# One place sooner: context sum and root between the query's products, a tile's column sums ahead of the bias columns, and the first weights rounded on VectorE

## The chip, the cores and the metric

The kernel runs on one core of a Trainium2 chip. A core has five engines that run side by side, each with its own instruction queue, in order: TensorE (PE in the rows; its weight loads are PEld), VectorE (DVE), ScalarE (ACT), GpSimd (POOL) and SyncE (SP), which here issues most of the transfers. Engines wait for each other at semaphores. The metric is the device time of one execution in microseconds, lower is better.

## The reference

One layer of a diffusion backbone over 512 latent tokens and 256 context tokens with 1024 channels. Only the start matters here:

```python
mod = silu(c) @ w_mod + b_mod                      # six pieces; here shift and scale 1
mod_c = silu(c_ctx) @ w_mod + b_mod
h_lat = rmsnorm(x, norm1_g) * (1 + sc1) + sh1      # 512 x 1024
h_ctx = rmsnorm(ctx, norm1_g) * (1 + csc1) + csh1  # 256 x 1024
p_lat, p_ctx = h_lat @ w_in, h_ctx @ w_in
```

The columns of `w_in` feed a state-space mixer, a windowed attention whose latent queries also read the context's keys and values, and two gates. A merge, a gated convolution FFN and a last norm follow.

## The kernel before

**Products in two parts.** Every fp32 operand of a large product is split into a rounded part `hi` and a remainder `lo`, and a product is three TensorE passes: hi x hi, hi x lo, lo x hi. Weights are split by `split(r, n, hi, lo)` (L148): a ScalarE copy rounds into `hi` (L149), a VectorE subtraction gives `lo` (L150). Activations are channel-major, in eight tiles of 128 channels: `hlh`, `hll` for the latent tokens, `hch`, `hcl` for the context.

**The opening stage.** Eight tiles j = 0 to 7 of the input are worked on while their modulation weights `wm` (two transfers of 512 KB for each j) and the first gate's weights `w0` (five column blocks of 128) stream in on SP's queue. For each tile the steps of the order below are:

- `A`: sixteen small products of `silu(c)` with the modulation weights (L370), copied by ScalarE to a row `tm` (L372); here also `split_w(j)` splits the gate weights of the tile into `w0h` and `w0l`.
- `B`: four small products that turn the row into columns (L380), and two ScalarE steps that make the tile's scale `a` (L381) and shift `s` (L382) from them. These are the column sums of the tile.
- `H`: the tile's operand. For j below 4 it is `x` times the scale alone (`scaled`: ScalarE `ah` L409, VectorE `al` L410), as the norm's root is not there yet; from j = 4 on it is the whole norm (`norm`: VectorE L400 on `xsb`, ScalarE `hlh` L401, VectorE `hll` L402).
- `Pj:ab`: the products of tile j with the gate's column blocks a to b-1 (L418), accumulated in five PSUM banks.
- `Z`: for j below 4, the shift's own product with the gate weights (L427), a bias.
- `N`: the full norm of tiles 0 to 3, later.
- `sum_l`, `put_l`: TensorE sums the squares (L237), VectorE and GpSimd make the root (L247, L248), TensorE spreads it over the partitions (L254) and ScalarE copies it out as `r_l` (L273). `scale_a`, `scale_b` multiply the five banks by it (L455). `sum_c` and `put_c` do the same for the context: squares `sq_c`, `sq_d` (ScalarE L393, VectorE L395 into `te`), then the sum, the root and `r_c`.
- `rows`, `cols`: the gate's bias, taken out of PSUM as rows by ScalarE (L459, L460) and turned into columns by small products (L464, L465), which ScalarE copies to `gb` (L467).
- `hold`, `keep`: products that nobody reads.

**What sets the order.** TensorE's order in this stage is the written one. The other engines' instructions are placed by the framework's planner, from its own estimate of what is ready when, with the program's order as rank. After the last tile comes the query's first gemm, still in written order: eight steps k of three products (L193, L194, L196). `gemm` takes one entry from the list `BETWEEN` after steps 1, 4 and 7:

```python
if BETWEEN and k % 3 == 1:
    BETWEEN.pop(0)()
```

Behind it, ScalarE's tanh (L533) empties the five gate banks, `norm` makes the context's `hch`, `hcl` from `r_c`, and `k_step` multiplies the key weights with latent and context operands; the planner orders TensorE again there. The query's rotation reads its bank through four ScalarE swaps (L612) and a VectorE product (L616), and the second query tile and the values follow. The attention and the later stages have orders of their own, written out or made by a planner inside the kernel with fixed costs.

Of the kernel before, what the change touches and what calls it, by code (L numbers as in the profile page):

```python
# [13 lines left out]
ALU = mybir.AluOpType  # L14
# [25 lines left out]
def raw(ap):  # L40
    return ap.bitcast(F32)
# [3 lines left out]
def tile_hybrid_layer(  # L45
# [33 lines left out]
    V, S, G, T = nc.vector, nc.scalar, nc.gpsimd, nc.tensor  # L79
# [28 lines left out]
    def accb():  # L108
        return bank("acc")
# [37 lines left out]

    def split(r, n, hi, lo):  # L148
        S.copy(hi[:, :n], r[:, :n])  # L149
        V.tensor_tensor(lo[:, :n], r[:, :n], raw(hi[:, :n]), ALU.subtract)  # L150

    ELSEWHERE = {}

    def load(key):
        r, n = load_raw(key)
        if key[0] == "m":
            return r
        if key in ELSEWHERE:
            hi, lo = ELSEWHERE[key]()
            split(r, n, hi, lo)  # L160
            return hi, lo
        hi = wpool.tile([P, 1024], F32R, tag="whi", name="whi", bufs=2)
        lo = wpool.tile([P, 1024], F32R, tag="wlo", name="wlo", bufs=2)
        split(r, n, hi, lo)
        return hi, lo
# [19 lines left out]
    BETWEEN = []  # L185

    def gemm(targets, w, nk=KT, m=P, k0=0, first=True, last=True, ks=None):
        hi, lo = w
        for k in range(nk) if ks is None else ks:
            wh, wl = hi[:, k * m : (k + 1) * m], lo[:, k * m : (k + 1) * m]  # L190
            a, b = first and k == 0, last and k == nk - 1
            for ps, xh, xl in targets:
                T.matmul(ps, wh, xh[:, k0 + k, :], start=a, stop=False)  # L193
                T.matmul(ps, wh, xl[:, k0 + k, :], start=False, stop=False)  # L194
            for ps, xh, xl in targets:
                T.matmul(ps, wl, xh[:, k0 + k, :], start=False, stop=b)  # L196
            if BETWEEN and k % 3 == 1:
                BETWEEN.pop(0)()
# [13 lines left out]
    half = cpool.tile([P, NV - V_CW], F32, name="half")  # L212
# [87 lines left out]
    with tc.tile_pool(name="spool", bufs=1) as sp:  # L300
# [15 lines left out]
        def load_w0(j):  # L316
            r = sp.tile([P, 640], F32, tag="w0", name="w0", bufs=4)
            nc.sync.dma_start(r, w0[j])
            return r
# [11 lines left out]
        w0_raw = {0: load_w0(0)}  # L331
# [31 lines left out]
        def mod_rows(j):  # L363

            for u in range(2):
                i = 2 * j + u
                w = mod_raw.pop(i) if i in mod_raw else load_mod(i)
                for k in range(4):
                    z = slice(32 * k, 32 * k + 32)
                    T.matmul(pmod[z, 0:256], csil32[:, 4 * u + k, :], w[:, k, :], start=u == 0, stop=u == 1)  # L370
            row = tmp("tm")[:, :256]
            tc.keep_in_program_order(S.copy(row, pmod[:, 0:256]))  # L372
            if j + 1 < KT and j + 1 not in w0_raw:
                w0_raw[j + 1] = load_w0(j + 1)
            W[j] = split_w(j)
            return row
# [7 lines left out]
        def split_w(j):  # L384
            hi = sp.tile([P, 640], F32R, tag="w0h", name="w0h", bufs=2)
            lo = sp.tile([P, 640], F32R, tag="w0l", name="w0l", bufs=2)
            split(w0_raw[j], 640, hi, lo)
            return hi, lo

        def squares(x_, q, n, ks):  # L390
            for k in ks:
                sq = tmp(("ta", "tb")[k % 2])[:, :n] if k else q
                tc.keep_in_program_order(S.activation(sq, x_[:, k, :], AF.Square))  # L393
                if k:
                    V.tensor_tensor(q, q, sq, ALU.add)  # L395
# [17 lines left out]
        def products(j, w, h, gs=range(NG)):  # L413

            st, en = j == 0, j in (NU - 1, KT - 1)
            for a, b in ((0, 0), (0, 1), (1, 0)):
                for i in gs:
                    T.matmul(  # L418
                        pg[i], w[a][:, i * P : (i + 1) * P], h[b], start=st and a + b == 0, stop=en and a == 1,
                        skip_group_check=True,  # L420
                    )
# [10 lines left out]
        r, W, H = {}, {}, {}  # L432
# [16 lines left out]
        def hold(n):  # L449
            for _ in range(n):  # L450
                T.matmul(unread[:, :256], still[:, :P], still, start=True, stop=True)
# [21 lines left out]
        def load_next():  # L473
# [9 lines left out]
        rows = {}  # L483
# [7 lines left out]
        calls = {  # L491
            "sq_0": lambda: squares(xs_, ssq, L, range(1)),
            "sq_1": lambda: squares(xs_, ssq, L, range(1, 2)),
            "sq_2": lambda: squares(xs_, ssq, L, range(2, 4)),
            "sq_3": lambda: squares(xs_, ssq, L, range(4, 8)),
            "hold": lambda: hold(18),
            "keep": lambda: hold(6),
            "sq_c": lambda: squares(xc_, cq, LC, range(4)),
            "sq_d": lambda: squares(xc_, cq, LC, range(4, 8)),
# [13 lines left out]

        order = """
            hold A0 keep B0 H0 sq_0 keep Z0 P0:02 A1 P0:23 B1 H1 sq_1 P0:35 A2 P1:02 B2 H2 sq_2 P1:25 Z1 P2:02 sq_3 A3 P2:23 B3 H3
            P2:35 sum_l Z2 P3:02 A4 put_l P3:23 B4 H4 P3:35 scale_a Z3 scale_b rows A5 half P4:02 cols P4:23 B5 H5 P4:35 A6
            P5:02 B6 H6 P5:24 A7 ctx N0 P5:45 B7 H7 next P6:02 N1 P6:25 N2 P7:02 sq_c N3 P7:25 sq_d
        """
        with tc.manual_schedule(engines={mybir.EngineType.PE}):
            for what in order.split():  # L520
                if what in calls:
                    calls[what]()
                elif what[0] == "P":
                    j = int(what[1])
                    products(j, W[j], H[j], range(int(what[3]), int(what[4])))
                else:
                    does[what[0]](int(what[1]))
            first["q"] = accb()
            BETWEEN.extend([lambda: None, calls["sum_c"], calls["put_c"]])
            gemm([LAT(first["q"])], first["w"][0])  # L530
        for i in range(NG):
            t = tmp("tb")
# [1625 lines left out]
```

## Time and profile before

| | before |
|---|---|
| median of 3 runs | 1234.06 us (1233.9 to 1234.56) |
| the profiled execution | 1233.26 us |
| its span, first to last instruction | 1231.3 us |
| granted TensorE clock, mean | 0.998 |
| TensorE busy | 1217.0 us (99% of the span) |
| VectorE, ScalarE, GpSimd busy | 913.9, 687.9, 168.0 us |

The profile is one execution. A row of the timeline has the start in us from the span's start, the duration, engine, line, operation, output and inputs with their shapes, the count where neighbours are merged, and in brackets the idle time of the engine before it with what ended it. A row of the list of waits has the engine, tile and line that waited, the one it waited for, then us in total, times and the longest. A row of the table of windows has the window's bounds, its length, the busy time (and count) of TensorE, its weight loads, VectorE, ScalarE and GpSimd, then the granted clock, the DMA engines' busy share and GB/s. A row of the chain has start, duration and the work that the end of the span is traced back to. Ends of products are modelled and overlap, so the steps between starts say more than durations.

### The profile page before, as it was taken

To read this page: it belongs to the slowest core of one execution; us is meant where nothing else is said; L and a number is where in the kernel's file an instruction comes from. 1 tells how busy PE (TensorE), PEld (TensorE's weight loads), DVE (VectorE), ACT (ScalarE), POOL (GpSimd) and SP (SyncE) were. 2 spreads that over 40 slices of the span, in tenths; PEclk is the share of its full clock that TensorE was granted. 3 is DMA by queue.
4 is the path that set the end of the run, shared out by engine and by line. 5 is a ranking of instruction groups with operands and counts; after the bars stand their busy time and mean duration, and the time that the engine had idled before them with its cause. 6 is when DMAs were issued, how large, how long until landed. Compare 5 with 4: busy or idle time off the path is not lost.

```text
span 1231.3 us, 17460 instructions
## 1 busy us (share of the span) xinstructions
PE 1217.0 (99%) x6328; PEld 996.2 (81%) x6328; DVE 913.9 (74%) x1483; ACT 687.9 (56%) x1303; POOL 168.0 (14%) x174
## 2 busy tenths in 40 slices
PE   9999999999999999999999999999999999999997
PEld 6788888888878877777777778888988888888886
DVE  4767887888664698697886786677688788886566
ACT  4657788888444646566586563223544444445543
POOL 0000111121100043233351530000200000000000
PEclk9999999999999999999999999999999999999999
DMA  9653668877946235445346466677144444457785
GB/s 357 254 146 89 211 191 193 222 191 204 229 148 213 87 122 144 127 127 183 128 134 203 135 200 226 226 249 233 47 164 150 145 151 150 153 170 250 240 318 183
DMA packets 108630, 224.65 MB, mean 182 GB/s; under 512 B 9600, under 2 KB 48832, under 8 KB 108544
## 3 DMA queue, kind: packets, MB, share of 16 engines
q1 hardware_dynamic: 101056, 197.32, 48.6%
q0 software_dynamic: 6912, 25.17, 8.8%
q8 instruction: 50, 0.82, 0.3%
q10 hardware_dynamic: 576, 1.05, 0.2%
q14 instruction: 36, 0.29, 0.1%
HBM read 193.29 MB, written 49.87 MB: 197 GB/s over the span
## 4 chain that ended last, share of the span: by engine, by line
PE 93%; DVE 3%; ACT 2%; DMA 1%; issue 0%; SPq 0%; POOLq 0%; ACTq 0%; DVEq 0%
PE acc L193 19%; PE acc L194 19%; PE acc L196 19%; PE acc L1915 3%; PE acc L1913 3%; PE acc L1914 3%; PE score L807 3%; PE po L856 3%; PE pt L843 2%; PE mis L418 2%; PE mis L1476 2%; PE mis L1381 2%; PE acc L926 1%; PE acc L927 1%; PE acc L928 1%; PE mis L1399 1%
## 5 line engine op out<-in xcount | busy, mean ns | idle before, releaser
L193 PE MATMUL acc<-hlh,whi 128*128 128x512 f32 x488 | 199.3, 408 | 0.0
L150 DVE TENSOR_TENSOR wlo<-wraw,whi 128x1024 fp32r<-128x1024 f32 (+2 forms) x119 | 143.5, 1207 | 72.3 <-ACT whi L149 62.7
L149 ACT CAST whi<-wraw 128x1024 fp32r<-128x1024 f32 (+2 forms) x119 | 122.8, 1033 | 128.2 <-PE acc L194 80.1
L196 PE MATMUL acc<-hlh,wlo 128*128 128x512 f32 x488 | 191.4, 392 | 0.0
L194 PE MATMUL acc<-hll,whi 128*128 128x512 f32 x488 | 190.7, 391 | 0.0
L193 PE MATMUL acc<-mh,whi 128*128 128x512 f32 x360 | 141.0, 392 | 0.0
L196 PE MATMUL acc<-mh,wlo 128*128 128x512 f32 x360 | 140.1, 389 | 0.0
L194 PE MATMUL acc<-ml,whi 128*128 128x512 f32 x360 | 140.0, 389 | 0.0
L196 PEld LDWEIGHTS acc<-hlh,wlo 128*128 128x128 f32 x488 | 91.6, 188 | 20.3
L194 PEld LDWEIGHTS acc<-hll,whi 128*128 128x128 f32 x488 | 91.9, 188 | 17.5 <-issue 1.7
L193 PEld LDWEIGHTS acc<-hlh,whi 128*128 128x128 f32 x488 | 91.8, 188 | 17.5 <-issue 2.2
L193 PEld LDWEIGHTS acc<-mh,whi 128*128 128x128 f32 x360 | 67.6, 188 | 14.4 <-issue 0.5
L194 PEld LDWEIGHTS acc<-ml,whi 128*128 128x128 f32 x360 | 67.6, 188 | 14.3 <-issue 0.5
L196 PEld LDWEIGHTS acc<-mh,wlo 128*128 128x128 f32 x360 | 67.6, 188 | 14.2
L816 DVE CUSTOM_DVE_ANT_0 p<-score,winm,nsink 128x512 f32<-128x512 f32 (+1 forms) x64 | 51.8, 810 | 15.1 <-PE score L807 13.6
L1264 DVE SCALAR_TENSOR_TENSOR ta<-acc,half,ta 128x511 f32<-128x511 f32 (+1 forms) x66 | 43.8, 663 | 25.7 <-ACT ta L1263 25.6
L1263 ACT ACTIVATE ta<-acc,half 128x512 f32<-128x512 f32 (+1 forms) x66 | 46.7, 708 | 27.0 <-PE acc L196 25.7
L1271 ACT ACTIVATE tb<-ta 128x512 f32<-128x512 f32 (+1 forms) x44 | 23.5, 534 | 65.2 <-DVE ta L1265 59.2
L823 ACT ACTIVATE p<-p,mneg 128x512 f32<-128x512 f32 (+1 forms) x64 | 49.7, 777 | 15.3 <-DVE mneg L816 14.7
L1383 POOL TENSOR_TENSOR st<-st,eT 128x512 f32<-128x512 f32 x24 | 33.5, 1396 | 170.2 <-ACT st L1401 161.9
L193 PE MATMUL acc<-hch,whi 128*128 128x256 f32 x176 | 54.5, 310 | 1.2 <-ACT hch L401 1.2
L851 DVE TENSOR_TENSOR ptl<-pt,pth 128x512 fp32r<-128x512 f32 x72 | 47.5, 686 | 8.6 <-ACT pth L847 7.8
(501 smaller groups left out, 2969.4 us busy)
## 6 DMA issues: line engine op xcount, KB each, us to landing
wraw<-wup SPq DMA_DIRECT2D x44, 512.0 KB, 3.6
wt_d<-wdn POOLq DMA_DIRECT2D x36, 512.0 KB, 7.5
fb<-cs_d SPq DMA_DIRECT2D x32, 512.0 KB, 6.4
wraw<-wm SPq DMA_DIRECT2D x32, 512.0 KB, 4.2
wraw<-wx SPq DMA_DIRECT2D x24, 512.0 KB, 3.6
wraw<-wt_d SPq DMA_DIRECT2D x20, 512.0 KB, 4.2
sp_d<-te SPq DMA_DIRECT2D x33, 256.0 KB, 2.3
wm<-wm SPq DMA_DIRECT2D x16, 512.0 KB, 7.7
```

The costliest lines, as they stand in the source:

```text
L149: S.copy(hi[:, :n], r[:, :n])
L150: V.tensor_tensor(lo[:, :n], r[:, :n], raw(hi[:, :n]), ALU.subtract)
L193: T.matmul(ps, wh, xh[:, k0 + k, :], start=a, stop=False)
L194: T.matmul(ps, wh, xl[:, k0 + k, :], start=False, stop=False)
L196: T.matmul(ps, wl, xh[:, k0 + k, :], start=False, stop=b)
L807: T.matmul(ps[:, o : o + len(z) * P], Q[h][:, b * P : (b + 1) * P], k[:, j, z[0] * P : (z[-1] + 1) * P], start=v == 0 and o % 512 in (0, P ...
L816: V.tensor_tensor_reduce(p[:, :w], d["ps"][i][:, o0 : o0 + w], m, op0=ALU.add, op1=ALU.min, scale=1.0, scalar=nsink[:, h : h + 1], accum_o ...
L823: S.activation(p, p, AF.Exp, bias=d["mneg"][:, i : i + 1], scale=-1.0, accum_out=d["den"][:, i : i + 1])
L851: V.tensor_tensor(d["ptl"][x], d["pt"][x], raw(d["pth"][x]), ALU.subtract)
L856: T.matmul(d["po"], vst[:, cols[x], j, :], d[y][x], start=x == 0 and y == "pth", stop=x == c - 1 and y == "ptl")
L1263: S.activation(o[:, :n], ps[:, :n], AF.Identity, scale=hcol(base_w, stride + i), bias=hcol(base_b, i))
L1264: V.scalar_tensor_tensor(o[:, 1:n], ps[:, 0 : n - 1], hcol(base_w, i), o[:, 1:n], ALU.mult, ALU.add)
```

## The change

Three edits, all in the opening stage:

1. The gate weights of tile 0 are rounded by VectorE instead of ScalarE (`split_first`); tiles 1 to 7 as before.
2. In TensorE's written order the sixth tile's `B5` and `H5` come directly behind `P4:02`, ahead of `cols`, and `P4:23` and `P4:35` become one group `P4:25`.
3. The empty first entry of `BETWEEN` goes, so that the context's sum and root come behind step 1 of the query's gemm and the spread behind step 4, instead of 4 and 7.

```diff
+    def split_first(r, n, hi, lo):
+        V.tensor_copy(hi[:, :n], r[:, :n])
+        V.tensor_tensor(lo[:, :n], r[:, :n], raw(hi[:, :n]), ALU.subtract)
+
...
-            split(w0_raw[j], 640, hi, lo)
+            (split if j else split_first)(w0_raw[j], 640, hi, lo)
...
-            P2:35 sum_l Z2 P3:02 A4 put_l P3:23 B4 H4 P3:35 scale_a Z3 scale_b rows A5 half P4:02 cols P4:23 B5 H5 P4:35 A6
+            P2:35 sum_l Z2 P3:02 A4 put_l P3:23 B4 H4 P3:35 scale_a Z3 scale_b rows A5 half P4:02 B5 H5 cols P4:25 A6
             P5:02 B6 H6 P5:24 A7 ctx N0 P5:45 B7 H7 next P6:02 N1 P6:25 N2 P7:02 sq_c N3 P7:25 sq_d
...
-            BETWEEN.extend([lambda: None, calls["sum_c"], calls["put_c"]])
+            BETWEEN.extend([calls["sum_c"], calls["put_c"]])
```

## The prediction

> **What bounds the kernel now.** I read the page's totals first, then the list of what TensorE (PE in the rows) waited for in the first 110 us, then the timeline at each of those waits. The totals:
>
> ```profile
> span 1231.3 us, 17460 instructions
> PE 1217.0 (99%) x6328; PEld 996.2 (81%) x6328; DVE 913.9 (74%) x1483; ACT 687.9 (56%) x1303; POOL 168.0 (14%) x174
> ```
>
> TensorE is busy for 1217.0 of 1231.3 us, so a change that leaves its products alone can win only what lies in its gaps. The change touches the stretch up to the query's first products, and the gaps there are few. The list's longest (microseconds in total, times, longest); the others that matter stand with their rows below:
>
> ```profile
> PE acc L193 <- ACT hch L401: 1.2, 1, 1.2
> ```
>
> Each of the change's three parts aims at one of them: the VectorE rounding at the wait for `ah` near 10 us, the earlier sums of the sixth tile at the wait for `hlh` near 42 us, the earlier context sum and root at the wait for `hch` near 70 us.
>
> **Part A, first weights rounded on VectorE.** One copy of 128x640 leaves ScalarE (ACT) and one of the same size joins VectorE (DVE). The other seven tiles keep their ScalarE copy.
>
> ```profile
> 3.07 0.43 SPq L318 DMA_DIRECT2D w<-w  x1
> w<-w SPq DMA_DIRECT2D x1, 320.0 KB, 4.6
> 8.63 0.72 ACT L149 CAST w0h<-w 128x640 fp32r<-128x640 f32 x1
> 8.94 0.62 PE L427 MATMUL acc<-w,s 128*32 128x256 f32 x6
> 9.24 0.72 ACT L409 ACTIVATE ah<-xsb,a 128x512 fp32r<-128x512 f32 x1
> 9.38 0.83 DVE L150 TENSOR_TENSOR w0l<-w,w0h 128x640 fp32r<-128x640 f32 x1 [2.55 <-ACT w0h L149]
> 10.12 0.75 DVE L410 SCALAR_TENSOR_TENSOR al<-xsb,a,ah 128x512 fp32r<-128x512 f32 x1
> 10.02 0.73 PE L418 MATMUL mis<-ah,w0h 128*128 128x512 f32 x2 [0.46 <-ACT ah L409]
> 10.92 0.73 PE L418 MATMUL mis<-al,w0h 128*128 128x512 f32 x2 [0.17 <-DVE al L410]
> ```
>
> The first column is the start, the second the duration. The weights land at 3.07 + 4.6 = 7.7 us, and VectorE stands idle for 2.55 us before its subtraction at 9.38. So it can round from 7.7 us. No row shows a rounding copy of this size on VectorE. The nearest are the subtraction of the same 640 columns, 0.83 us, as the upper end, and nothing as the lower. I take 0.83, which is the same engine and the same size: rounding ends by 8.6 and the subtraction by 9.4. At either end both are done before `al` could start, so the price does not enter the sum. (The Trainium skill, VectorE: DVE Perf Modes, gives an fp32 copy in SBUF two elements a cycle and 58 cycles of fixed cost: an estimate of 378 cycles at 0.96 GHz, 0.39 us. The sum by it would be the same.)
>
> On ScalarE `ah` then takes the place of the cast: it moves from 9.24 to about 8.63, 0.61 earlier, and ends at 9.35. TensorE's bias products (L427) hold it until 9.56. The products with `ah` so start at 9.56 instead of 10.02, and `al` starts at about 9.45 and ends at 10.2, so that its products start at 10.26 instead of 10.92. The local gain is 0.66 us, and what is behind on ScalarE also moves up. But it lasts only to the fourth tile's modulation products:
>
> ```profile
> 20.00:30.00 10.00, 9.97 (x70) 6.32 (x72) 7.28 (x12) 5.82 (x12) 1.39 (x1) 1.00 0.98 387
> 23.00 1.30 PE L370 MATMUL acc<-wm,csil 128*32 128x256 f32 x16
> 40.21 1.07 PE L370 MATMUL acc<-wm,csil 128*32 128x256 f32 x16
> 23.67 0.16 PEld L370 LDWEIGHTS acc<-wm,csil 128*32 128x32 f32 x8 [0.51 <-DMA wm<-wm]
> ```
>
> From 20 to 30 us the DMA engines are busy for 0.98 of the time. The sixteen products at 23.00 take 1.30 us where a later group takes 1.07, because the second half waited for its weights, which let it go at 23.67. TensorE is already 0.23 us too early there. If it comes 0.66 earlier, it waits 0.66 longer for the same transfer, since that transfer sits in a queue whose engines have no time left. I take 0 for part A, with 0.66 as the upper end (the transfer would have to land sooner by as much) and 0 as the lower, since the moved work has idle time on VectorE as its cover; without that cover it would cost its 0.83.
>
> **Part B, the sixth tile's column sums before the bias columns.** Tile 5's four small products (B5, L380) move ahead of the bias columns (L464, L465), and P4:23 and P4:35 become one group P4:25.
>
> ```profile
> 36.96 0.28 PE L464 MATMUL acc<-sel,tc 96*128 96x3 f32 x2
> ...
> 37.48 0.50 PE L418 MATMUL mis<-hlh,w0h 128*128 128x512 f32 x1
> ...
> 38.28 0.51 PE L380 MATMUL acc<-sel,tm 128*128 128x2 f32 x4
> 38.65 0.71 PE L418 MATMUL mis<-hlh,w0h 128*128 128x512 f32 x2
> 39.19 0.63 PE L418 MATMUL mis<-hll,w0h 128*128 128x512 f32 x2
> ...
> 41.87 0.73 PE L418 MATMUL mis<-hlh,w0h 128*128 128x512 f32 x2 [0.59 <-ACT hlh L401]
> 42.82 0.50 PE L418 MATMUL mis<-hll,w0h 128*128 128x512 f32 x1 [0.21 <-DVE hll L402]
> 39.86 0.73 ACT L149 CAST w0h<-w 128x640 fp32r<-128x640 f32 x1 [0.53 <-PE mis L418]
> 39.21 1.41 DVE L400 SCALAR_TENSOR_TENSOR xsb<-xsb,a,r_l 128x512 f32<-128x512 f32 x2 [0.76 <-ACT a L381]
> 48.09 7.11 PE mis L418 x30
> ```
>
> B5 starts at 36.96 instead of 38.28, 1.32 us sooner, and so does its scale `a`. VectorE, which stood idle for 0.76 us until `a` came, then does not wait, and `hlh` and `hll` of tile 5 can come 0.76 to 1.32 us sooner. TensorE's own time shrinks a little as well: the two groups took 37.48 to 38.28 (0.80) and 38.65 to 40.21 (1.56), together 2.36. The last row, from the chain, has thirty such products in one run at 7.11/30 = 0.237 each; nine at the 2.13 that this makes and about 0.07 of entry are 2.20. So P4:25 saves 0.16.
>
> The gap is larger than the marked idle time. A group of this kind needs 39.19 - 38.65 = 0.54 from its first product to its first with the low part. Before, the modulation products at 40.21 ended their issue at 41.28 (1.07 later), so the low part could have started at 41.28 + 0.54 = 41.82; it started at 42.82. That is 1.00 lost, and with the 0.16 the whole part is worth 1.16 us. The marks, 0.59 + 0.21, say 0.80. Here the page named Perfetto Trace Analysis of the Trainium skill bears, in Identifying the Most-Contended Engine: matmul busy time is a poor measure because pipelined instructions look smaller in the trace. This trace agrees: by the marks this part would be worth 0.80 + 0.16 = 0.96, by starts 1.16.
>
> I take 1.0 of it: the ScalarE cast at 39.86 waits for TensorE itself, so it moves up by little more than the 0.16, and if the planner leaves it ahead of tile 5's `hlh`, a few tenths of the wait stay. What is behind the moved work: the two `gb` copies on ScalarE now follow tile 5's scale and shift, and nothing reads `gb` before the gate's tanh, which follows the last of these products; SP and POOL get nothing new, no DMA moves. Ends: 0, if `hll` stays late because VectorE takes other norms first, and 1.32, the whole shift of B5. The next cover is VectorE's own backlog between 40 and 50 us.
>
> **Part C, context sum and root one place sooner.** The query's gemm has eight steps of three products. The sum of squares moves from behind step 4 to behind step 1, the spread from behind step 7 to behind step 4: nine products each. At 0.23 a product (the second row, from the chain) that is 2.07 us.
>
> ```profile
> 55.12 0.43 DVE L395 TENSOR_TENSOR te<-te,tb 128x256 f32<-128x256 f32 x1
> 55.20 0.23 PE acc L193
> 58.47 0.50 PE L237 MATMUL acc<-rmsc,te 128*128 128x1 f32 x4
> 59.24 0.71 POOL L248 TENSOR_TENSOR rs<-ms,phalf 128x2 f32<-128x2 f32 x1 [29.67 <-DVE ms L247]
> 58.70 0.69 ACT L533 ACTIVATE tb<-mis,gb 128x512 f32<-128x512 f32 x1 [0.58 <-DMA ts_d<-tb]
> 61.01 0.38 PE L254 MATMUL acc<-ident,rs 128*128 128x128 f32 x2
> 60.97 1.05 ACT L149 CAST whi<-wraw 128x1024 fp32r<-128x1024 f32 x1 [1.58 <-PE acc L194]
> 61.93 0.37 ACT L273 COPY r_c<-acc 128x256 f32<-128x256 f32 x1
> 63.20 2.46 DVE L400 SCALAR_TENSOR_TENSOR xcb<-xcb,a,r_c 128x256 f32<-128x256 f32 x6
> 68.75 0.28 PE L196 MATMUL acc<-hch,wlo 128*128 128x256 f32 x1
> 70.22 0.39 PE L193 MATMUL acc<-hch,whi 128*128 128x256 f32 x1 [1.20 <-ACT hch L401]
> ```
>
> Alone, it puts the sum at 58.47 - 2.07 = 56.4 and the spread at 58.95, ending 59.3. The root, done 1.48 after the sum starts (59.24 + 0.71 - 58.47), still comes 1.06 before the spread, as before. Before, `r_c` was copied only at 61.93, since ScalarE had begun a 1.05 us cast at 60.97 just ahead of it. Now the spread ends in ScalarE's 1.58 us of idle time before that cast, so `r_c` is there at about 59.8 instead of 62.3: 2.5 sooner. VectorE then has sixteen context operations at 2.46/6 = 0.41 and one weight subtraction, at 0.83 x 1024/640 = 1.33 by size, 7.9 us in all, ending by 67.7; the context products want their seventh tile at 68.75 + 0.12 = 68.87, the 0.12 being half of the 0.23 that a product of twice the columns takes. So the stall, 70.22 - 68.87 = 1.35 by starts and 1.20 by the mark, should go. Ends: -0.2 (the last squares are added at 55.55, and with part B's shift TensorE asks for them at 55.4, so 0.2 may be lost where nothing else moves) and 1.35. I take 1.20, as the order of both engines there is the planner's.
>
> **The sum.** 0 + 1.0 + 1.2 = 2.2 us. From the profiled execution's own 1233.26 us that gives 1231.1; it lay 0.80 under the median of the runs shown, 1234.06, so on their level the forecast is 1231.9 us. Later stages keep TensorE busy to within a few tenths in each 10 us and follow orders that this change does not alter, so a gain here should reach the end. A change below 0.2% (2.47 us) can't be told from none by such runs.
>
> **The rivals.**
> - Part C only renames its wait: `r_c` still lands behind the tanh copies or the cast on ScalarE, or the planner hands the query's rope swaps the time won, and TensorE waits for `hch` as before. Against it is the 1.58 us gap on ScalarE; for it, that this order is not written by hand. Then part B's 1.0 alone remains: 1233.1 us.
> - Part A's 0.66 us is kept, because the transfer awaited at 23.67 lands sooner or a little of the wait there was TensorE's own start. Against it is the DMA share of 0.98. Then 2.2 + 0.66 = 2.86: 1231.2 us.
> - Slower: the context squares are not yet added when the sum's new place comes. Were the last two squares put behind the four gate tanh copies on ScalarE, they would come after those, 58.70 + 0.69 = 59.4, with two additions of 0.43 behind them: 60.3. TensorE would ask at 56.4 - 1.0 = 55.4 and wait 4.9, which loses more than the 2.2 won: 1234.06 - 2.2 + 4.9 = 1236.8 us. It decides against the change once the additions end after 55.4 + 2.2 = 57.6; before they ended at 55.55, which speaks against it.
>
> **How the numbers follow.** Both B and C as in the sum: 0.50, between 1231.2 and 1232.6, two fifths of it past 2.47 us of gain. C without effect: 0.22. A kept as well: 0.14. Squares late: 0.08. The remaining 0.06 is for an order of the planner that I don't foresee, half to each side. Faster by over 0.2%: 0.20 + 0.14 + 0.03 = 0.37; slower by over 0.2%: 0.08 + 0.03 = 0.11; within: 0.52. The range goes from A kept less the runs' own spread (0.66, from 1233.9 to 1234.56), 1230.5, to C without effect and B halved (0.5), plus that spread, 1234.2.
>
> **What would show it.** Right: no `ah` wait at 10 us, the wait for `wm` weights near 23.6 grown to about 0.9, no `hlh` or `hll` wait near 41, `r_c` before the 1.05 us cast, no `hch` wait, and every mark after 75 us moved up by about 2.2. Wrong: a TensorE wait for `te` at the sum, the `hch` wait still there, or the end of the fourth tile's modulation products earlier than 24.2.

## The result, and the profile after

| | before | after |
|---|---|---|
| median, 21 runs each, side by side | 1233.7 us (1232.9 to 1236.56) | 1231.95 us (1230.95 to 1233.47) |
| the profiled execution | 1233.26 us | 1232.22 us |
| its span | 1231.3 us | 1230.4 us |
| granted TensorE clock, mean | 0.998 | 0.998 |

The ratio is 0.9985, 95% interval 0.9979 to 0.9991: 1.75 us less by the medians. The interval does not reach 1, so the kernel is faster, but by less than the 0.2% from which on the prediction would call a change faster. The forecast was 1231.9 us and 2.2 us less, with a range of 1230.5 to 1234.2. Lines behind L150 carry numbers higher by 4 than before (L418 is L422, L193 is L197, and so on).

The totals of the changed kernel, and TensorE's waits in its first 110 us. The wait for `still` belongs to the products that nobody reads; it is the same before and after and is left aside here.

```profile
span 1230.4 us, 17460 instructions
PE 1218.5 (99%) x6328; PEld 996.3 (81%) x6328; DVE 914.1 (74%) x1484; ACT 687.0 (56%) x1302; POOL 167.9 (14%) x174
```

```profile
PE acc L455 <- POOL still L348: 1.1, 1, 1.1
PE acc L241 <- DVE nsink L485: 0.3, 1, 0.3
PE acc L374 <- DMA wm<-wm: 0.2, 1, 0.2
```

Of the waits that the three parts aim at (`ah`, `al`, `hlh`, `hll`, `hch`) none is left in the list. The 0.2 for the weights `wm` belongs to tile 3, near 24 us. A new one has come: L241, the context's sum, waits for VectorE. Its releaser is shown as `nsink`, the small VectorE operation right behind the last addition of squares; what the sum reads is `te`, that addition's output.

TensorE's timeline of the changed kernel at the places of the prediction:

```profile
10.23 0.73 PE L422 MATMUL mis<-ah,w0h 128*128 128x512 f32 x2
11.02 0.73 PE L422 MATMUL mis<-al,w0h 128*128 128x512 f32 x2
...
23.97 0.64 PE L374 MATMUL acc<-wm,csil 128*32 128x256 f32 x8 [0.24 <-DMA wm<-wm]
...
30.19 0.42 PE L374 MATMUL acc<-wm,csil 128*32 128x256 f32 x4
...
37.26 0.50 PE L384 MATMUL acc<-sel,tm 128*128 128x2 f32 x4
...
40.51 1.07 PE L374 MATMUL acc<-wm,csil 128*32 128x256 f32 x16
41.52 0.74 PE L422 MATMUL mis<-hlh,w0h 128*128 128x512 f32 x2
42.22 0.73 PE L422 MATMUL mis<-hll,w0h 128*128 128x512 f32 x2
...
45.20 1.07 PE L374 MATMUL acc<-wm,csil 128*32 128x256 f32 x16
...
54.58 0.40 PE L197 MATMUL acc<-hlh,whi 128*128 128x512 f32 x1
...
56.40 0.58 PE L241 MATMUL acc<-rmsc,te 128*128 128x1 f32 x4 [0.27 <-DVE nsink L485]
...
68.54 0.28 PE L197 MATMUL acc<-hch,whi 128*128 128x256 f32 x1
68.90 0.28 PE L197 MATMUL acc<-hch,whi 128*128 128x256 f32 x1
...
75.15 0.30 PE L693 MATMUL mis<-whi,hlh 128*128 128x320 f32 x1
```

And four rows of before that the prediction did not need:

```profile
29.89 0.42 PE L370 MATMUL acc<-wm,csil 128*32 128x256 f32 x4
45.79 1.07 PE L370 MATMUL acc<-wm,csil 128*32 128x256 f32 x16
55.03 0.40 PE L193 MATMUL acc<-hlh,whi 128*128 128x512 f32 x1
76.53 0.30 PE L689 MATMUL mis<-whi,hlh 128*128 128x320 f32 x1
```

These are the marks that all kernels below are read by. **A4** is the first of tile 4's modulation products (29.89 before, 30.19 after); some expectations call it the fourth tile's. **q** is the query's first product (55.03, 54.58), **V** the values' first product (76.53, 75.15). Before A4 the time depends on when the first transfers land, which differs between executions of one kernel. Between A4 and V TensorE waits for the other engines alone, in every trace here. From A4 to V it is 46.64 us before and 44.96 after: 1.68 less, close to the 1.75 of the medians. In this one execution A4 itself came 0.30 later than before, so the bare positions show less: V moved up by 1.38.

### The profile page after: what moved, and what is told of

Its sections match the earlier page's. It is cut to its first block, busy times and chain, and to the rows that moved or that the text cites. A ratio compares the mean times of both kernels' runs of the same rounds, so it can differ in the third digit from the quotient of the medians.

```text
span 1230.4 us, 17460 instructions
## 1 busy us (share of the span) xinstructions
PE 1218.5 (99%) x6328; PEld 996.3 (81%) x6328; DVE 914.1 (74%) x1484; ACT 687.0 (56%) x1302; POOL 167.9 (14%) x174
## 4 chain that ended last, share of the span: by engine, by line
PE 92%; DVE 3%; DMA 2%; ACT 2%; issue 1%; SPq 0%; POOLq 0%; ACTq 0%; DVEq 0%
PE acc L197 19%; PE acc L200 19%; PE acc L198 19%; PE acc L1919 3%; PE acc L1917 3%; PE acc L1918 3%; PE score L811 3%; PE po L860 3%; PE pt L847 2%; PE mis L1480 2%; PE mis L1385 2%; DMA wm<-wm 1%; PE mis L422 1%; PE acc L930 1%; PE acc L931 1%; PE acc L932 1%
## 5 line engine op out<-in xcount | busy, mean ns | idle before, releaser
L197 PE MATMUL acc<-hlh,whi 128*128 128x512 f32 x488 | 199.3, 408 | 0.0
L150 DVE TENSOR_TENSOR wlo<-wraw,whi 128x1024 fp32r<-128x1024 f32 (+2 forms) x119 | 143.4, 1207 | 71.9 <-ACT whi L149 62.2
L197 PE MATMUL acc<-mh,whi 128*128 128x512 f32 x360 | 141.0, 392 | 0.0
L197 PEld LDWEIGHTS acc<-hlh,whi 128*128 128x128 f32 x488 | 91.8, 188 | 17.5 <-issue 2.2
L197 PEld LDWEIGHTS acc<-mh,whi 128*128 128x128 f32 x360 | 67.6, 188 | 14.3 <-issue 0.5
L197 PE MATMUL acc<-hch,whi 128*128 128x256 f32 x176 | 54.4, 309 | 0.0
```

## The experiments

Each experiment is an edit of the changed kernel and ran in five rounds beside the kernel before. The median of before was 1233.92, 1233.82 and 1234.49 us in the three groups (a_alone to no_a; x_first to sum_at_2; squares1 to early_wm), so a kernel is compared by its ratio to the before of its own group.

| kernel | A4 to q | q to sum | q to V | A4 to V | less than before | median, us | ratio (95% interval) |
|---|---|---|---|---|---|---|---|
| before | 25.14 | 3.44 | 21.50 | 46.64 | | | |
| a_alone | 25.15 | 3.44 | 21.48 | 46.63 | 0.01 | 1233.87 | 0.9999 (0.9990 to 1.0008) |
| b_alone | 24.38 | 3.44 | 21.82 | 46.20 | 0.44 | 1233.47 | 0.9995 (0.9986 to 1.0004) |
| c_alone | 25.16 | 1.39 | 20.00 | 45.16 | 1.48 | 1232.32 | 0.9989 (0.9980 to 0.9998) |
| no_a (B and C) | 24.39 | 1.82 | 20.53 | 44.92 | 1.72 | 1232.05 | 0.9981 (0.9972 to 0.9990) |
| after (A, B, C) | 24.39 | 1.82 | 20.57 | 44.96 | 1.68 | 1231.95 | 0.9985 (0.9979 to 0.9991) |
| late_put | 24.38 | 1.81 | 22.09 | 46.47 | 0.17 | 1233.78 | 0.9998 (0.9989 to 1.0007) |
| squares1 | 24.69 | 1.40 | 20.04 | 44.73 | 1.91 | 1232.33 | 0.9986 (0.9977 to 0.9994) |
| six_squares | 24.39 | 1.39 | 20.01 | 44.40 | 2.24 | 1231.67 | 0.9977 (0.9968 to 0.9986) |
| early_wm | 24.39 | 1.82 | 20.50 | 44.89 | 1.75 | 1232.47 | 0.9984 (0.9976 to 0.9993) |

The intervals are about 1.1 us to each side, so the times alone separate few of these kernels. The distances of the marks carry the argument. Each kernel has one trace, but the distances repeat between kernels with the same order: A4 to q is 24.38 or 24.39 in every kernel of the table with part B and the squares as written, and 25.14 to 25.16 in every kernel without B. A4 to V is 44.89 to 44.96 in the three kernels that differ only ahead of A4 (no_a, after, early_wm). The times follow the distances as far as their intervals allow.

**Each part by itself.** The theory was the prediction's sum: 0 for A, about 1.0 for B, about 1.2 for C.

a_alone takes parts B and C back:

```diff
-... A5 half P4:02 B5 H5 cols P4:25 A6
+... A5 half P4:02 cols P4:23 B5 H5 P4:35 A6
-            BETWEEN.extend([calls["sum_c"], calls["put_c"]])
+            BETWEEN.extend([lambda: None, calls["sum_c"], calls["put_c"]])
```

> Only the first weights rounded on VectorE. Theory (the gain is taken back at the fourth tile's modulation weights): the products with the first tile start up to 0.66 us sooner, the sixteen modulation products that start near 23 us take longer than 1.3 us, and they end when the transfer lands, as before; 0 us, within 0.3 of the kernel before. Rival (the wait there was partly TensorE's own lateness): those products end sooner by 0.4 to 0.66 us and the time falls by as much.

b_alone takes A and C back:

```diff
-            (split if j else split_first)(w0_raw[j], 640, hi, lo)
+            split(w0_raw[j], 640, hi, lo)
-            BETWEEN.extend([calls["sum_c"], calls["put_c"]])
+            BETWEEN.extend([lambda: None, calls["sum_c"], calls["put_c"]])
```

> Only the sixth tile's column sums ahead of the bias columns. Theory: from the end of P4:02 to the seventh tile's column sums TensorE needs 6.5 us instead of 7.36, 0.9 less, and the time falls by 0.9 us; the wait for hch near 70 us stays at 1.2. Rival (VectorE's backlog from 40 to 50 us takes it back before the query's products): the query's first product starts less than 0.3 us sooner, and the time falls by less than 0.3.

c_alone takes A and B back:

```diff
-            (split if j else split_first)(w0_raw[j], 640, hi, lo)
+            split(w0_raw[j], 640, hi, lo)
-... A5 half P4:02 B5 H5 cols P4:25 A6
+... A5 half P4:02 cols P4:23 B5 H5 P4:35 A6
```

> Only the context's sum, root and spread one place sooner. Theory: without part B the sum comes at about 56.4 us, after the last squares are added at 55.55, so there is no wait at the sum, and the whole stall of 1.35 us by starts (1.2 by the mark) before the context's products goes: 1.2 to 1.35 us less. Rival (part C is worth the same alone as together, 0.9, as the wait at the sum comes from the planner's order and not from part B's shift): a wait of 0.2 to 0.4 us at the sum here too, and 0.9 us less.

no_a takes A back alone:

```diff
-            (split if j else split_first)(w0_raw[j], 640, hi, lo)
+            split(w0_raw[j], 640, hi, lo)
```

> The changed kernel with the first weights rounded on ScalarE again: parts B and C together. Theory (A is worth nothing): the same as the changed kernel, 1.7 us under the kernel before, and the same small wait at the sum. Rival (A keeps 0.66): only 1.1 us under the kernel before.

Measured: A changes nothing from A4 on (0.01 alone; beside B and C 1.68 with it and 1.72 without). But A acts ahead of A4, so these distances can't tell what it wins there, and its ratio alone, 0.9999, has an interval wider than the 0.66 us in question. This is taken up below. B brings the query 0.76 us sooner, with C or without, but alone it delivers only 0.44 at V. The wait for `hch` is gone there, and another stands in its place, from the list of waits of b_alone:

```profile
PE acc L197 <- DVE tb L620: 0.5, 1, 0.5
```

That is a product that wants the query's bank, which VectorE's rotation had not yet read. With the context's root where it was before, TensorE's earlier arrival partly became a wait for a different reader.

C alone delivers 1.48, and nothing waits at its sum. TensorE's timeline of c_alone, query and sum:

```profile
54.95 0.40 PE L197 MATMUL acc<-hlh,whi 128*128 128x512 f32 x1
...
56.33 0.50 PE L241 MATMUL acc<-rmsc,te 128*128 128x1 f32 x4
```

The sum stands 1.39 us behind the query, two steps of three products. In the changed kernel it stands 1.82 behind, with a marked wait of 0.27. B and C do not add: 0.76 and 1.48 would make 2.24 and the two together make 1.72. Two theories remained for the missing half microsecond: the squares are late for the sum, now that B brings TensorE there sooner; or the chain of context norms limits the two together wherever the sum stands. VectorE's timeline of the changed kernel ahead of the sum speaks for the squares:

```profile
53.71 1.22 DVE L150 TENSOR_TENSOR wlo<-wraw,whi 128x1024 fp32r<-128x1024 f32 x1
54.85 0.42 DVE L399 TENSOR_TENSOR te<-te,tb 128x256 f32<-128x256 f32 x1
55.30 0.42 DVE L399 TENSOR_TENSOR te<-te,ta 128x256 f32<-128x256 f32 x1
55.83 0.43 DVE L399 TENSOR_TENSOR te<-te,tb 128x256 f32<-128x256 f32 x1
```

The last addition ends at 56.26, while TensorE, by c_alone's 1.39, would have asked at 54.58 + 1.39 = 55.97.

**Two additions fewer.** six_squares leaves the last two context tiles out of the sum of squares:

```diff
-            "sq_d": lambda: squares(xc_, cq, LC, range(4, 8)),
+            "sq_d": lambda: squares(xc_, cq, LC, range(4, 6)),
```

> The last two context tiles are left out of the sum of squares (two squares on ScalarE, two additions on VectorE less), so that the values are not the reference's; nothing else is moved. Theory: with the last two additions gone (0.9 us) nothing but TensorE itself sets the sum, 1.39 us behind the query's first product instead of 1.82; the value's first product is 44.5 us behind the fourth tile's instead of 44.96 and the time about 1231.5 us, 0.4 under the changed kernel. So much is what the squares take from parts B and C together (0.90 and 1.48 alone, 1.68 to 1.72 together). Rival: the 0.43 us wait is only renamed; the next wait (the query's bank, the context's seventh tile, or another) takes it and the value's product stays 44.9 behind: then it is the chain of context norms, and not the squares, that bounds B and C together.

TensorE's timeline of six_squares:

```profile
54.08 0.39 PE L197 MATMUL acc<-hlh,whi 128*128 128x512 f32 x1
...
55.47 0.50 PE L241 MATMUL acc<-rmsc,te 128*128 128x1 f32 x4
```

The sum is back at 1.39, and A4 to V is 44.40: 2.24 less than before, exactly B's 0.76 plus C's 1.48. So the squares, and not the norms behind them, took the 0.52 to 0.56 from B and C together. The time went to 0.9977, though its interval overlaps that of the changed kernel.

**The squares sooner.** squares1 keeps all squares and starts the second group one product group earlier; only one square on ScalarE and one addition on VectorE change places with other work:

```diff
-... N1 P6:25 N2 P7:02 sq_c N3 P7:25 sq_d
+... N1 P6:25 sq_c N2 P7:02 sq_d N3 P7:25
```

> The second group of context squares is started one product group earlier; TensorE's order is that of the changed kernel, on ScalarE and VectorE one square and its addition move ahead of tile 7's two high parts and low parts. Theory (parts B and C together make TensorE ask for the sum before VectorE has added the squares, which costs 0.43 us by starts: 1.82 us from the query's first product to the sum where part C alone has 1.39): the addition fills VectorE's 0.42 us of idle time near 49.6, the last addition ends up to 0.35 us sooner, the sum stands 1.4 to 1.5 us behind the query's first product, and the value's first product 44.6 to 44.7 us behind the fourth tile's instead of 44.96: about 1231.6 us, 0.3 less than the changed kernel. Rival (the wait is set by the weights' subtractions ahead of the last additions, or the square on ScalarE delays tile 7's high part by its 0.31): the sum stays 1.8 behind the query, or a new wait at tile 7's products takes as much; time as the changed kernel or up to 0.3 more.

TensorE's timeline of squares1:

```profile
50.24 0.69 PE L422 MATMUL mis<-hlh,w0h 128*128 128x512 f32 x2
51.05 0.73 PE L422 MATMUL mis<-hll,w0h 128*128 128x512 f32 x2
...
54.18 0.39 PE L197 MATMUL acc<-hlh,whi 128*128 128x512 f32 x1
...
55.58 0.31 PE L241 MATMUL acc<-rmsc,te 128*128 128x1 f32 x2
```

Theory and rival were both partly right. The sum no longer waits (1.40), which gives 0.53 from q to V: 20.04, where c_alone has 20.00. All the squares are done here, so it is their lateness that costs, and not the work that six_squares leaves out. But tile 7's low part comes late: 0.81 us from its first product to its first with `hll` where no_a has 0.49 (50.37 to 50.86), and A4 to q grows by 0.30, the price of one square ahead of `hlh` on ScalarE. What is left is 0.23 at V, too little for the clock to show: 0.9986 against the changed kernel's 0.9985.

**The root late again.** late_put keeps the sum early and puts the spread back behind step 7:

```diff
-            BETWEEN.extend([calls["sum_c"], calls["put_c"]])
+            BETWEEN.extend([calls["sum_c"], lambda: None, calls["put_c"]])
```

> The sum stays behind the query's second step as in the changed kernel, the spread of the root goes back behind the eighth product group as before. Theory (what part C wins it wins by the root being spread into ScalarE's idle time): the copy of the root on ScalarE comes 2 us later and behind the first copies of the rope swap (0.5 us), near 61.5 to 62 instead of 59.4, the wait for the context's high part or for the query's bank is there again with 0.8 to 1.3 us, the value's first product stands 46.0 to 46.3 us behind the fourth tile's as with part B alone (46.20), and the time is 1233.2 us, 1.2 over the changed kernel. Rival (the sum's place alone is enough, since the root stands ready): the value's product stays at 45.0 and the time at 1232.0.

ScalarE's timeline of late_put, its TensorE row with the new wait, and the row of the changed kernel for comparison:

```profile
60.25 0.59 ACT L616 ACTIVATE ta<-acc 32x512 f32<-32x512 f32 x1 [1.20 <-PE acc L200]
60.87 0.37 ACT L277 COPY r_c<-acc 128x256 f32<-128x256 f32 x1
...
70.52 0.50 PE L200 MATMUL acc<-hlh,wlo 128*128 128x512 f32 x1 [0.77 <-DVE wlo L150]
```

```profile
59.42 0.37 ACT L277 COPY r_c<-acc 128x256 f32<-128x256 f32 x1 [2.39 <-PE acc L258]
```

The root's copy stands behind the first swap of the query's rotation, as expected, 2.43 us later than in the changed kernel when both are taken from A4 (60.87 - 29.21 against 59.42 - 30.19). VectorE then works on the context until late, comes to the next weights' subtraction 1.61 us later (40.04 us behind A4 against 38.43), and TensorE waits for `wlo`. A wait returns, though a different one from the two that were named, and the gain is 0.17 at V and nothing measurable in time. From q to V it is even slower than b_alone, which has sum and spread at their old places (22.09 against 21.82). So part C wins by the spread's place. The sum's earlier place, which the earlier spread needs, wins nothing by itself.

**A sum that nothing waits for.** sum_at_2 puts the sum one step later (behind step 2) and the spread behind step 5, through a switch in `gemm` that is set for the query alone:

```diff
-            if BETWEEN and k % 3 == 1:
+            if BETWEEN and k % 3 == (WHEN[0] if WHEN else 1):
```

> The changed kernel with the context's sum and root behind step 2 of the query's gemm and the spread behind step 5, one step later than the change puts them. Theory (part C as changed trades 0.44 us by starts for a wait at the sum, since part B moves TensorE up more than VectorE's last squares): no wait at the sum, r_c still before the next ScalarE cast, the context's products still without a wait: 0.3 to 0.45 us less than the changed kernel. Rival (the later spread costs what the sum's wait did): a wait for hch or for the query's bank of the same size near 69 us, and the same time as the changed kernel.

It took 1236.13 us, ratio 1.0017 (1.0008 to 1.0026): slower, and neither theory had that. The sum no longer waits, but the planner ordered everything behind it anew (the values now stand before the second query tile). Its list of waits has two new ones:

```profile
PE acc L197 <- ACT whi L149: 1.8, 1, 1.8
PE mis L695 <- ACT whi L149: 0.7, 1, 0.7
```

So this run says nothing on the sum's best place, only that a move by one step there can give the planner another order, 4 us worse than the changed kernel's.

**Where part A goes.** Six traces have part A and the queue's order of the changed kernel (after, a_alone, squares1, six_squares, late_put, sum_at_2), four have not (before, b_alone, c_alone, no_a). The products with `al` start at 10.62 on average with A (10.21 to 11.02) and at 10.91 without (10.81 to 11.05): 0.29 us sooner, not 0.66. Tile 3's last modulation product starts at 23.65 with A (23.24 to 24.23) and at 23.76 without (23.62 to 23.93): 0.1 is left. A4 itself lies at 29.62 with A (29.21 to 30.19) and at 29.72 without (29.58 to 29.89). The traces with A lie up to 0.98 us apart there, so ten traces make a gain of 0.66 unlikely, and can't tell a few tenths from none. The timeline of the changed kernel near 9 us, and the issue-to-landing time (the last number, us) of its first weights:

```profile
8.73 0.49 DVE L153 CAST w0h<-w 128x640 fp32r<-128x640 f32 x1 [1.69 <-DMA w<-w]
9.45 0.72 ACT L413 ACTIVATE ah<-xsb,a 128x512 fp32r<-128x512 f32 x1 [0.18 <-DMA xsb<-xT]
```

```profile
w<-w SPq DMA_DIRECT2D x1, 320.0 KB, 5.6
```

The weights took 4.6 us from issue to landing in the trace that the prediction read, and 4.8 to 5.6 in the other nine. At 5.6 VectorE's rounding starts at 8.73, not at 7.7, and `ah` waits for `x`, which is next in the queue. Four runs tried the two transfers that A meets.

early_wm asks for tile 3's modulation weights ahead of its data:

```diff
-        load_x(3)
         mod_raw.update({i: load_mod(i) for i in (6, 7)})
+        load_x(3)
```

> Of the fourth tile the first modulation weights are asked for ahead of its data, on the same queue; all other orders are those of the changed kernel. Theory (part A's gain is lost to these weights where the first transfers land early, and to the first transfers where they land late): the wait among the tile's sixteen products goes, its last product stands 0.70 us behind its first instead of 1.1 to 1.3; worth 0.0 us at the end if the first data landed 5.5 us or more from its issue, up to 0.4 us (1231.6) if it landed before 5.0. Rival: the data of the fourth tile, now behind, lands late for its own products, and 0.3 to 0.6 us is lost.

TensorE's and ScalarE's rows of early_wm:

```profile
22.58 1.07 PE L374 MATMUL acc<-wm,csil 128*32 128x256 f32 x16
23.29 0.63 ACT L397 ACTIVATE ta<-xsb 128x512 f32<-128x512 f32 x1 [1.71 <-DMA xsb<-xT]
24.75 0.61 PE L384 MATMUL acc<-sel,tm 128*128 128x2 f32 x4 [0.21 <-ACT tm L376]
```

The rival was right on the loss: the sixteen products run without a break, but ScalarE now waits 1.71 us for the tile's data, its copy of `tm` comes behind these squares, and TensorE needs 6.44 us from tile 3's last modulation product (23.27) to A4, where the other kernels need 5.96. Since three of the six traces with A had no break there either, the move's own gain is not shown.

x_first asks for the first weights and the first data ahead of the identity and the vectors, x_first_wm moves tile 3's weights as well, and x_first_wm_no_a is that without part A:

```diff
-        nc.sync.dma_start(ident, ident_d)
-        nc.sync.dma_start(vec[:, :V_N2], vecs[:, :V_N2])
         w0_raw = {0: load_w0(0)}
         load_tile(0)
+        nc.sync.dma_start(ident, ident_d)
+        nc.sync.dma_start(vec[:, :V_N2], vecs[:, :V_N2])
```

> The changed kernel with the first gate weights and the first tile of x issued ahead of the identity and the vectors (92 KB together) on SP. Theory (part A is first held by the landing of the first x tile near 9.2 us, then once more by the tile-3 modulation weights near 23.4): the first tile's low-part products start at about 10.3 us instead of 10.8, TensorE reaches the tile-3 modulation products 0.3 to 0.5 us sooner, at about 22.5, and still ends them at about 23.6; time within 0.3 of the changed kernel. Rival (only the first transfer held it): those products end 0.3 to 0.5 sooner and the time falls by as much.

> As x_first, and the tile-3 modulation weights are issued ahead of the last 512 KB of x. Theory: both transfers that held part A are now early; the tile-3 modulation products start at about 22.5 and end at 23.3 or sooner, 0.3 to 0.6 us before the changed kernel's, and the time is 0.3 to 0.6 us less than the changed kernel's, unless the late x tiles hold the squares (then TensorE waits at the latent sum near 27 us). Rival (the place is not bound by these transfers): no shift there.

> As x_first_wm, with the first weights rounded on ScalarE again. Theory: the first tile's low-part products wait for the ScalarE cast as in the kernel before (start at about 10.8), TensorE reaches the tile-3 modulation products near 22.9, and the time is 0.3 to 0.5 us more than x_first_wm's. Rival (part A is worth nothing even where no transfer holds it): the same time and the same marks as x_first_wm.

They took 1233.44, 1232.93 and 1233.85 us, ratios 0.9991 (0.9982 to 1.0000), 0.9990 (0.9981 to 0.9999) and 0.9998 (0.9989 to 1.0007). The move failed in its aim. The identity and the vectors then landed late, and the column sums of the first tile waited, in x_first:

```profile
PE acc L384 <- DVE bp L362: 1.0, 1, 1.0
```

Its tile 3 begins at 23.26, no sooner than the changed kernel's 23.09. With and without A, A4 to V is the same, 44.89 (x_first_wm) and 44.87 (x_first_wm_no_a). Ahead of A4 the second trace is 2.1 us later and the medians differ by 0.92 us with overlapping intervals, so whether A matters in that order of the queue stays open.

## Why the prediction was right, and which steps were not

**The sum.** 0 + 1.0 + 1.2 = 2.2 was forecast; 1.75 by the medians, 1.68 from A4 to V. The terms of B and C as measured there are 0.76 + 1.48 - 0.56 = 1.68, the last being what the squares take (44.96 - 44.40). A's term lies ahead of A4 and is not in that distance. The time of 1231.95 us, so close to 1231.9, owes 0.36 us to the level: the before of these runs was 1233.7 and not 1234.06.

**Part A, 0.** The value fits the ten traces (0.1 at A4, well inside their spread), and the reason holds only in part. The step "it can round from 7.7 us" used one landing time, the earliest of ten. In the other traces most of the local 0.66 was lost to the first weights and the first data, before tile 3's weights could take the rest; on average 0.29 arrived at the products with `al`, and 0.1 was left behind tile 3's. The loss at `wm` did not grow from 0.23 to 0.9: in the changed kernel the sixteen products took 0.44 longer than without a break (1.14 from the first start to the last, against 0.70), with a mark of 0.24. Where TensorE came earliest, in the trace of sum_at_2 (22.29), it did wait for these weights and ended where the kernels without A do (23.61 against 23.62 to 23.93), as the prediction said. But late_put came at 22.55, did not wait and ended at 23.24, so the landing of these weights moves between executions as well. The sign "earlier than 24.2" can't sort the kernels either, since the products end earlier in some traces without A too. The rival that A keeps 0.66 is made unlikely by the ten traces. It is not excluded by the time of a_alone, whose interval of 0.9990 to 1.0008 holds it. The rounding itself took 0.49 us, between the bounds of 0 and 0.83. The Trainium skill, VectorE: DVE Perf Modes, in its section on the TRN2 errata, adds to the 58 cycles of its table that the measured fixed term is about 150. With that, 150 + 320 cycles at 0.96 GHz are an estimate of 0.49 us, and this trace agrees; the 0.39 from the table is too low here.

**Part B, 1.0.** Its place was right: no marked wait for `hlh` or `hll` is left near 41 us. From the first product of tile 4 to tile 5's first low part it was 7.39 us before (35.43 to 42.82) and 6.49 in b_alone (35.12 to 41.61): 0.90, all of it from the wait. The term of 0.16 that P4:25 should save was mis-sized: the group takes 0.07 less than its two parts did (38.22 to 40.51 is 2.29, not 2.20), the bias columns ahead of it take 0.08 longer, and from the moved products to tile 6's modulation products TensorE needs 3.25 us before (36.96 to 40.21) as after (37.26 to 40.51). Of the 0.90, 0.76 arrives at the query. 0.13 is lost at tile 7, whose first four products (two with `hlh`, two with `hll`) take 1.07 us in the changed kernel (50.95 to 52.02) and 0.94 before (51.53 to 52.47), with no mark at the low part. That the 1.0 lies near 0.90 is in part luck: the prediction took 0.16 off its 1.16 for the order of the ScalarE cast, and what was missing was the saving in P4:25. The prediction also saw its trace agree that pipelined products look smaller. Its rows show the opposite: a product of the query has a record of 0.40 us (at 55.03) where the next one starts after 0.23, so records overlap and cover part of a gap, and the marks say less (0.80) than the starts (1.00).

**Part C, 1.2.** The mechanism was right: `r_c` at 59.42 instead of 61.93 and no wait for `hch`. It is worth 1.48 alone, above the 1.35 that was computed for the stall by starts; where the other 0.13 comes from stays open. Where the sum went wrong is the lower end of this part: "the last squares are added at 55.55, and with part B's shift TensorE asks for them at 55.4, so 0.2 may be lost where nothing else moves". That was the right place and a loss in the right direction, but it was put at nothing in the sum, and it measured 0.43 at the sum of squares and 0.56 at V. The wait for `te` that the prediction named as a sign of being wrong is this one. The step took the additions to stay where they were while TensorE came sooner. They came later: their end stands 25.66 us behind A4 before (55.55 - 29.89) and 26.07 in the changed kernel (56.26 - 30.19). Part B does this: it is 25.67 in c_alone (29.78 to 55.45), 26.07 in no_a (29.61 to 55.68) and 26.05 in b_alone (29.58 to 55.63). VectorE's timeline of c_alone shows the difference in its order:

```profile
50.16 0.42 DVE L399 TENSOR_TENSOR te<-te,tb 128x256 f32<-128x256 f32 x1
50.57 0.75 DVE L406 SCALAR_TENSOR_TENSOR hll<-xsb,s,hlh 128x512 fp32r<-128x512 f32 x1
51.24 0.42 DVE L399 TENSOR_TENSOR te<-te,ta 128x256 f32<-128x256 f32 x1
51.58 2.36 DVE L150 TENSOR_TENSOR wlo<-wraw,whi 128x1024 fp32r<-128x1024 f32 x2
...
55.03 0.42 DVE L399 TENSOR_TENSOR te<-te,tb 128x256 f32<-128x256 f32 x1
```

Four of its seven additions are done before the two weights' subtractions. With part B, alone or with C, the planner has three there, a fourth between the subtractions, and three behind, and the last one ends 0.4 us later.

**The rivals.** "Part C only renames its wait" did not come, but late_put shows that it was near: with the spread 2 us later the root's copy falls behind a swap on ScalarE, and the gain goes. "Squares late" is what happened, at a tenth of the feared 4.9 us. The planner did not put the last squares behind the tanh copies; they were late behind VectorE's other work.

**Marks behind 75 us.** "Every mark moved up by about 2.2" is wrong for this execution: V came 1.38 sooner, the last product 1.00 (1223.03 to 1222.03). Of the difference to 1.68, 0.30 is the late start. Near 355 us another 0.34 is lost: from V to the transposes of `de` (L1157 in the changed kernel) it is 280.07 us in before and 280.41 in the changed kernel. In other traces this distance is near 280.1 (b_alone, no_a, six_squares) or near 280.4 (a_alone, c_alone, late_put, squares1, early_wm), with no part of the change that sorts them. What decides it stays open. "Later stages keep TensorE busy to within a few tenths" has an exception too: 9.02 of the 10 us from 540 to 550 in the trace of before.

## What to carry to other kernels

When several waits are removed one behind the other, work out each one's arrival with the shifts of the others in it: a producer that was just in time (55.55 for a reader at 55.4) turns late when another edit brings the reader sooner, and that difference belongs into the sum. Measure edits of a microsecond between two marks of one engine, behind the last transfer that anything waits for: between kernels with the same order A4 to q repeated to 0.02 us here and A4 to V to 0.07, where the ratios had an interval of about 1.1 us to each side. Such marks say nothing of an edit that acts ahead of the first of them, as part A does. And an edit that starts from a transfer's landing needs that landing from several executions before its gain is counted.

## What was not expected of the hardware

The same transfer of the first gate weights, 320 KB issued at 3.06 or 3.07 us on a queue with the same order ahead of it, landed 4.6 to 5.6 us after its issue in ten traces. This spread of 1.0 us is more than the 0.66 of part A. A4, where all ten have TensorE at work on the same product, lay between 29.21 and 30.19.
